# A two-block network in float32 on one core: float32 products of attention weights and values in block 2, a new order of the beginning, products of constants in waits, and late inputs of block 1 moved

## The chip, the core and the metric

The kernel runs on one core of one Trainium2 chip. TensorE (PE in the profile) makes the products, VectorE (DVE), ScalarE (ACT) and GpSimd (POOL) do the elementwise work, and SyncE (SP) issues nearly all DMAs. Each engine works off its instructions in one order that is fixed when the kernel is built. The metric is the time of one execution in microseconds (us), from the chip.

## What is computed

Two transformer-like blocks work on a latent sequence of 256 tokens (LAT) and a context of 256 tokens (CTX), both 1024 wide, in float32. Each block has two layers; each layer is an FFN, a mixer and a second FFN, and each of these three stands behind a norm that is scaled and shifted by "mods" (products of silu(c) with a large matrix). The mixers are a convolution of width 31, neighbourhood attention, attention with a latent key and value (MLA) beside windowed heads with a sink (SWA), and a state-space layer (S5).

```python
x = first_block(x, c, ctx, ...)          # FFN, conv, FFN; FFN, neighbourhood attention, FFN; norm
return second_block(x, c_2, ctx_2, ...)  # FFN, MLA + SWA, FFN; FFN, S5, FFN

def ffn_sublayer(h, m, j, g_pre, g_post, w13, w2):
    a = modulate(h, g_pre, m[3 * j], m[3 * j + 1])     # rmsnorm(h, g) * (1 + scale) + shift
    return h + FFN_RES * m[3 * j + 2] * rmsnorm(swiglu(a, w13, w2), g_post)

def softmax_attention(q, k, v, scale):
    s = jnp.einsum('bqhd,bkhd->bhqk', q, k) * scale
    return jnp.einsum('bhqk,bkhd->bqhd', jax.nn.softmax(s, axis=-1), v)
```

## The kernel before

All activations lie transposed, 1024 features as eight tiles of 128 partitions, 256 columns a stream. A product of two float32 matrices is made as three fast products of parts that were rounded beforehand: high times high, low times high, high times low (`mm`, L109, makes every product; `gemm` strings them together). ScalarE writes a high part (`hh` of activations at L693, `wh` of weights at L183, `th` in attention at L1587), VectorE the low one as the difference (`hl` L696, `wl` L188, `tl` L1588). Weights come in 1 MB pieces on SyncE's queue (`raw`), are converted, and wait in five slots; `pump` starts the next conversion when a slot comes free.

The stages follow one another: f100, conv, f102, f110, na, f112 of block 1, then f200, attn, f202, f210, s5, f212 of block 2 (an f is an FFN: pairs of gate and up tiles `gu`, then down tiles `pd`). Between two stages stands a norm: squares are summed up on ScalarE and VectorE, TensorE sums them over the partitions (`ssq`), GpSimd takes the power -1/2 (`rr`, L268), TensorE spreads it (`bc`), and VectorE and ScalarE make `nt`, `hh` and `hl`. Such steps are held in a `Chain` and sent in when a running clock of TensorE's work (`pe_t`) has gone on far enough; what is not sent by then is forced (`force`).

A `Task` is background work that is sent in the same way, a step for so many ns of TensorE's work. One of them, `pre` (`s5_pre`), makes the tables of S5 for eight d in two halves each, long before S5 needs them: rotations `E` (L2165 to L2172), `vw` (L2073 to L2085) and `ow` (L2110 to L2120) on GpSimd, small products `pvt` and `kp` on TensorE, copies on ScalarE and VectorE, and DMAs to tables `dE`, `dT`, `dK`, `dV`, `dO` in DRAM. It is handed to f100, f102 and f110 as `side`: an FFN starts it at its beginning and stops it at its end, and what is left is drained before na (L2511). The order on each engine is then set by a scheduler that takes instructions by the place in the program and by when a simulated clock says that they are ready.

In na (L1173) LAT's half of the projections `pq`, `pk`, `pv` comes first, CTX's behind it. A bias `vb` is loaded (L1232) and added to the values (`vt`, L1246). Behind na the second block's context is loaded into CTX's tile (L500). In conv TensorE does some of the taps with diagonal matrices `dgw` that ScalarE writes (L1004). In attn (L1531) `turn` transposes softmax weights and splits them into `th` and `tl`, and `pv` multiplies them by split values, three products for each pair of tiles.

Of the kernel before, what the change touches and what calls it, by code (L numbers as in the profile page):

```python
# [13 lines left out]
D = 1024  # L14
# [9 lines left out]
class Acc:  # L24
    def __init__(self, tag):
        self.tag, self.t, self.pend, self.ps = tag, None, None, None

# [9 lines left out]
class Chain:  # L37
    def __init__(self, k):
        self.k = k
        self.steps = []  # L40
        self.t0 = k.pe_t
        k.chains.append(self)
# [35 lines left out]
class Core:  # L78
    def __init__(self, ctx, tc, ap):
# [3 lines left out]
        self.n_mm, self.marks, self.pin = 0, [], None  # L83
        self.chains = []
# [16 lines left out]
        self.dma_max, self.dma_behind = 1 << 30, False  # L101
# [6 lines left out]
    def mm(self, out, lhsT, rhs, start, stop, cost, **kw):  # L108
# [7 lines left out]
        return ins  # L116

# [29 lines left out]
    def force(self, c):  # L147
        was, self.ticking = self.ticking, True
        c.force()
        self.ticking = was  # L150

# [18 lines left out]
    def pump(self):  # L170
        while self.n_cv < min(len(self.pieces), self.n_rel + NBUF):
# [71 lines left out]
    def rstd(self, ch, acc, ncol, eps, cb, d1=900, d2=1500, inv=None, parts=False, pin=0, keep=None):  # L243

        nc = self.nc
        if isinstance(acc, Acc):
            self.flush(acc)

        def s1():
# [19 lines left out]

            def s2():  # L270
                bc = self.psa.tile([128, 512], F32, tag="a", name="bc")
# [4 lines left out]
                cb(bc[:, :ncol * 128])  # L276
            ch.steps.insert(0, (d2, s2))
        ch.steps.append((d1, s1))

    def square(self, src, acc, first):  # L280
        if first:
# [190 lines left out]
class Net(Core):  # L472
    def setup(self):
# [3 lines left out]
        nc.sync.dma_start(out=self.vec, in_=ap["vecs"])  # L477
# [11 lines left out]
        self.x = {}  # L489
        self.acc = {}  # L490
        self.modv = {}
# [6 lines left out]
    def load_x(self, s, name):  # L498
        t = self.xp.tile([128, KT, T], F32, tag=f"x{s}", name=f"x{s}")
        self.nc.sync.dma_start(out=t, in_=self.ap[name])  # L500
        self.x[s] = t

# [47 lines left out]
    def begin(self, room):  # L550
# [13 lines left out]
        self.load_x(LAT, "x")  # L564
        self.load_x(CTX, "ctx")
        tl = {}

        def load(k):
            tl[k] = self.mwp.tile([128, D], F32, tag="mw", name="mw")
            nc.sync.dma_start(out=tl[k], in_=self.ap["mw1"][0, 8 + k])  # L570
            for i in range(2):
                nc.sync.dma_start(out=room[i][k].rearrange("p (j m) -> p j m", j=4), in_=self.ap["mshift"][k][:, 4 * i:4 * i + 4])
        self._dma()
        load(0)
# [5 lines left out]
        bcs, acc = {}, {}  # L580
        psh = [self.psm.tile([128, 512], F32, tag="m", name="psh"), self.psa.tile([128, 512], F32, tag="a", name="psh")]
        for s in S2:
            t = self.mwp.tile([128, D], F32, tag=f"cb{s}", name=f"cb{s}", bufs=1)
            for i in range(2):
                ps = self.psm.tile([128, 512], F32, tag="m", name="cbp")
                self.mm(ps, self.ones[0:1, :], room[i][6 + s][0:1, :], True, True, 858)
# [944 lines left out]
    def attn2(self, ready, finish):  # L1531
# [3 lines left out]
        with ExitStack() as es:  # L1535
# [200 lines left out]
            def pv(H, c):  # L1736
# [15 lines left out]
                if c == 2:  # L1752
                    low(1)
# [854 lines left out]
```

## Time and profile before

| | us |
|---|---|
| median of 3 runs | 3609.77 |
| lowest and highest | 3609.4, 3611.73 |
| profiled execution | 3612.36 |
| its span | 3610.5 |

The profile has the busy time of each engine, the chain of work that ended last (followed back from the last instruction, each step to what released it), groups of instructions by line, the timeline of one engine, and the busy time in windows of the span. PEclk is the granted clock of TensorE as a share of 2.4 GHz; it has two levels, 2.4 and 1.2 GHz. Times are us from the start of the span unless marked ns.

### The profile page before, as it was taken

Reading aid. Unit: us, or ns where it says so; the run is one execution under the profiler, and the core shown is the slowest. Engines: PE = TensorE matmul, PEld = TensorE weight load, DVE = VectorE, ACT = ScalarE, POOL = GpSimd, SP = SyncE. Lnnn points to the kernel's source line nnn. Section 1 sums busy time; section 2 is a strip of 40 time slices with the busy share of each in tenths; the row PEclk is TensorE's granted clock in tenths of the full one; section 3 lists DMA queues with packets and bytes.
Section 4 is the critical chain, followed back from the end, with each engine's and each line's share of the span. In section 5 each row is a group of like instructions: output and inputs, shape, how many; then the busy total and the mean of one; then the engine's idle time right before and its main releaser. Section 6 shows DMA issues by size and latency. Waiting matters only on the chain.

```text
span 3610.5 us, 54700 instructions
## 1 busy us (share of the span) xinstructions
PE 3482.7 (96%) x21248; PEld 3056.4 (85%) x21248; DVE 2590.3 (72%) x4487; ACT 1389.1 (38%) x2428; POOL 749.8 (21%) x870
## 2 busy tenths in 40 slices
PE   8999998999999999999999999889999999999898
PEld 7888867888898888989998889779888988897898
DVE  8987697876586765768987766878887633368655
ACT  4222444422242323554443234655322432244443
POOL 5100001577657772000000001211000100014000
PEclk9999999999999999999999999999999999999899
DMA  7555211455454774236755542014557332238353
GB/s 260 200 189 197 71 59 48 162 190 186 164 169 170 257 242 138 92 120 235 262 187 188 182 145 97 34 50 153 208 206 247 134 124 94 102 120 300 121 197 119
DMA packets 157835, 579.35 MB, mean 160 GB/s; under 512 B 25220, under 2 KB 56708, under 8 KB 117896
## 3 DMA queue, kind: packets, MB, share of 16 engines
q1 hardware_dynamic: 157576, 575.86, 45.8%
q8 instruction: 167, 2.74, 0.3%
q14 instruction: 92, 0.75, 0.1%
HBM read 546.50 MB, written 29.29 MB: 159 GB/s over the span
## 4 chain that ended last, share of the span: by engine, by line
PE 89%; DVE 7%; ACT 2%; issue 1%; POOL 1%; DMA 0%; SPq 0%; POOLq 0%; DVEq 0%; ACTq 0%
PE gu L109 46%; PE pd L109 24%; PE pj L109 8%; PE po L109 2%; PE ptap L109 1%; PE pv L109 1%; PE pk L109 1%; PE ps L109 1%; DVE wl L188 1%; PE ssq L109 1%; PE pT L109 1%; PE pq L109 1%; PE bc L109 1%; DVE ry L2291 0%; DVE jk L612 0%
## 5 line engine op out<-in xcount | busy, mean ns | idle before, releaser
L183 ACT ACTIVATE wh<-raw 128x1024 fp32r<-128x1024 f32 (+1 forms) x679 | 700.8, 1038 | 1581.4 <-PE gu L109 911.7
L188 DVE TENSOR_TENSOR wl<-raw,wh 128x1024 fp32r<-128x1024 f32 (+1 forms) x677 | 839.3, 1244 | 358.5 <-ACT wh L183 348.2
L109 PE MATMUL gu<-hl,wh 128*128 128x512 f32 (+1 forms) x3136 | 1083.8, 347 | 5.6 <-DVE hl L696 4.6
L109 PE MATMUL gu<-hh,wh 128*128 128x512 f32 (+1 forms) x3136 | 1076.9, 348 | 10.0 <-ACT hh L693 6.2
L109 PE MATMUL gu<-hh,wl 128*128 128x512 f32 (+1 forms) x3136 | 1082.0, 346 | 0.0
L538 DVE CUSTOM_DVE_ANT_0 jk<-mw,cb,vec 128x1024 bf16<-128x1024 f32 x480 | 639.0, 1331 | 73.2 <-DMA mw<-in_mw_dram 68.4
L109 PEld LDWEIGHTS gu<-hl,wh 128*128 128x128 f32 x3136 | 600.7, 192 | 78.2 <-DVE hl L696 6.0
L109 PEld LDWEIGHTS gu<-hh,wh 128*128 128x128 f32 x3136 | 596.9, 192 | 81.6 <-ACT hh L693 7.6
L109 PEld LDWEIGHTS gu<-hh,wl 128*128 128x128 f32 x3136 | 600.7, 192 | 70.3 <-issue 1.0
L109 PE MATMUL pd<-Hl,wh 128*128 128x256 f32 (+1 forms) x1696 | 561.8, 332 | 0.0
L109 PE MATMUL pd<-Hh,wl 128*128 128x256 f32 (+1 forms) x1696 | 561.0, 332 | 0.0
L109 PE MATMUL pd<-Hh,wh 128*128 128x256 f32 (+1 forms) x1696 | 559.0, 331 | 0.0
L268 POOL TENSOR_TENSOR rr<-rv,mhalf 128x2 f32<-128x2 f32 (+1 forms) x34 | 28.9, 850 | 1852.9 <-DVE rv L266 1796.4
L109 PEld LDWEIGHTS pd<-Hl,wh 128*128 128x128 f32 x1696 | 322.0, 190 | 30.2 <-issue 0.4
L109 PEld LDWEIGHTS pd<-Hh,wl 128*128 128x128 f32 x1696 | 321.9, 190 | 30.2 <-issue 0.4
L109 PEld LDWEIGHTS pd<-Hh,wh 128*128 128x128 f32 x1696 | 321.5, 190 | 29.9
L779 DVE TENSOR_TENSOR gu<-sg,gu 128x512 f32<-128x512 f32 (+1 forms) x196 | 113.4, 579 | 192.6 <-PE gu L109 191.6
L109 PE MATMUL pj<-hh,wh 128*128 128x256 f32 (+1 forms) x736 | 226.3, 322 | 15.4 <-ACT hh L693 9.0
L109 PE MATMUL pj<-hl,wh 128*128 128x256 f32 (+1 forms) x736 | 231.2, 318 | 1.1 <-DVE hl L1089 1.0
L109 PE MATMUL pj<-hh,wl 128*128 128x256 f32 (+1 forms) x736 | 228.5, 316 | 1.1 <-DVE wl L188 1.1
L109 PEld LDWEIGHTS pj<-hh,wh 128*128 128x128 f32 x736 | 142.0, 200 | 25.8 <-ACT hh L693 9.9
L109 PEld LDWEIGHTS pj<-hl,wh 128*128 128x128 f32 x736 | 146.8, 200 | 9.0 <-issue 1.7
(425 smaller groups left out, 4332.1 us busy)
## 6 DMA issues: line engine op xcount, KB each, us to landing
raw<-in_gu_dram SPq DMA_DIRECT2D x186, 1024.0 KB, 4.9
mw<-in_mw_dram SPq DMA_DIRECT2D x280, 512.0 KB, 4.6
raw<-in_dn2b_dram SPq DMA_DIRECT2D x38, 1024.0 KB, 4.7
raw<-in_dn1b_dram SPq DMA_DIRECT2D x32, 1024.0 KB, 5.3
raw<-in_dn1a_dram SPq DMA_DIRECT2D x16, 768.0 KB, 4.4
raw<-in_pw_dram SPq DMA_DIRECT2D x12, 1024.0 KB, 4.7
raw<-in_dn2a_dram SPq DMA_DIRECT2D x16, 768.0 KB, 4.3
dO<-ow SPq DMA_DIRECT2D x32, 256.0 KB, 2.6
```

The costliest lines, as they stand in the source:

```text
L109: ins = self.last_mm = self.nc.tensor.matmul(out=out, lhsT=lhsT, rhs=rhs, start=start, stop=stop, **kw)
L183: ins = nc.scalar.activation(out=h2, in_=r, func=AF.Copy)
L188: self.low_p = lambda eng=eng, l2=l2, r=r, h2=h2: eng.tensor_sub(l2, r, h2.bitcast(F32))
L268: nc.gpsimd.tensor_tensor(r[:, :ncol], v[:, :ncol], self.mhalf[:, :ncol], ALU.pow)
L538: self.behind_pe(nc.vector.tensor_tensor_reduce(out=jk, in0=tl[i], in1=self.cb[s], scale=1.0, scalar=self.V(f"mod_b{b}{l}")[:, j:j + 1], o ...
L779: nc.vector.tensor_mul(pr[:, :n], sg[:, :n], pu[:, :n])
```

## The change

Six things are edited; the diff is cut to its core.

- *Beginning.* x is loaded first, the vector table later; the norm steps of both streams are interleaved with the silus, and the first call of `pump` moves behind the first tile.
- *Products of constants.* `warm` puts float32 products of the 128 x 128 identity with itself into places where TensorE waits at norms: 112 in all.
- *`side`* starts in f102 and f110 ahead of the sixth tile pair.
- *conv.* The `dgw` activations are held behind what TensorE was last given.
- *na.* The bias's first load is written at the beginning of na, the load of `ctx_2` is held behind TensorE's last product, and `cv_max` puts off conversions of weights at na's end.
- *attn.* Transposed weights and values stay float32 and are multiplied in one float32 product; two heads share one tile, which is split once.

```diff
+    def warm(self, ps, ns, last=None):
+        for _ in range(int(ns / 215)):
+            ins = self.nc.tensor.matmul(out=ps[:, 256:384], lhsT=self.ident, rhs=self.ident, start=True, stop=True)
+            self.behind(ins, self.last_mm)
...
+            self.last_mm = self.pin = ins
...
+    def forced(self, c, late=0, least=0):
+        self.force(c, late)
+        if c.spare is not None:
+            self.warm(c.spare, max(1400 - (self.pe_t - c.t2), least), c.last)
...
@@ rstd
+                if self.late:
+                    self.warm(ps, 2800 + self.late - (self.pe_t - at))
...
             def s2():
+                n = 1700 - (self.pe_t - t1)
+                if at is not None and n > 215:
+                    self.warm(self.psa.tile([128, 512], F32, tag="a", name="idle"), n)
...
@@ begin
-        self.load_x(LAT, "x")
         self.load_x(CTX, "ctx")
+        nc.sync.dma_start(out=self.vec, in_=self.ap["vecs"])
...
+        sums(LAT)
+        first_step(ch[LAT])
+        silu(LAT)
+        sums(CTX)
+        self.force(ch[LAT])
+        first_step(ch[CTX])
+        silu(CTX)
+        shift(0)
+        self.force(ch[CTX])
+        scale(0)
         self.dma_max = 2
-        self.pump()
-        shift(0)
-        scale(0)
         for k in range(8):
...
+            if k == 0:
+                self.pump()
...
@@ ffn
             def background():
                 nonlocal task
-                if side is not None and not side.done:
+                if begin is not None and not side.done:
                     self.start(side)
...
-                            self.force(ready[s])
+                            self.forced(ready[s], late, 860 if two and b == 2 and s == streams[0] else 0)
+                            if self.cv_max < 1 << 30:
+                                self.cv_max = 1 << 30
+                                self.pump()
...
+                        if g == 0 and f == n1 + 1 and side is not None and not side.done and side not in self.tasks:
+                            self.start(side)
                         gu([(self.take(), self.take())], f, 0, N)
...
@@ conv
-                    nc.scalar.activation(out=dg, in_=self.ident, func=AF.Copy, scale=w(ek[len(dgs)]))
+                    self.behind_pe(nc.scalar.activation(out=dg, in_=self.ident, func=AF.Copy, scale=w(ek[len(dgs)])))
...
+                    if m == 1 and s == LAT:
+                        self.warm(ps, 1500)
...
@@ na
+            def vbias(g):
+                vb[g] = n2.tile([128, T], F32, tag="vb", name="vb", bufs=1)
+                nc.sync.dma_start(out=vb[g], in_=self.ap["vbias"][g * T:(g + 1) * T].partition_broadcast(128))
+            vbias(0)
...
+                self.cv_max = self.n_take + KT - 3 + 2
...
@@ joint_norm
+        self.warm(ps, 3600)
...
         for r in rs:
+            self.warm(self.psa.tile([128, 512], F32, tag="a", name="idle"), 1200 if r is rs[0] else 400)
...
+        self.warm(ps, 1500)
...
@@ attn2
-                split(th.rearrange("p a q -> p (a q)"), tl.rearrange("p a q -> p (a q)"), ps)
-                H["t", c] = (th, tl)
+                nc.scalar.activation(out=th.rearrange("p a q -> p (a q)"), in_=ps, func=AF.Copy)
+                H["t", c] = th
...
+                o = po[r:r + 64, :T] if c < 2 else po[r:r + 64, T:]
+                for i in range(2):
+                    self.mm(o, H["v"](2 * c + i if c < 2 else 2 + i), H["t", c][:, i, :], i == 0 and c != 1, i == 1 and c != 0, 429)
...
@@ s5
+                        if (b, m) == (0, 1) and d in (0, 7):
+                            self.warm(self.psa.tile([128, 512], F32, tag="a", name="idle"), 1900)
...
+        self.warm(self.psa.tile([128, 512], F32, tag="a", name="idle"), 1900)
         for d in range(2):
             glu_part(d, range(4, KT))
...
@@ network
-        self.load_x(CTX, "ctx_2")
+        self.behind_pe(self.load_x(CTX, "ctx_2"))
...
-        self.ffn(1, (LAT,), ready, gates(1, 1, 2, (LAT,)), final, work=(norm_and_mods(), 61))
+        self.ffn(1, (LAT,), ready, gates(1, 1, 2, (LAT,)), final, work=(norm_and_mods(), 61), late=1000)
```

How the order of instructions changes is shown at three places. A row has the line, the operation, out<-in with the program's names, the shape and a count. Lines are those of each kernel; before's L2110 to L2172 are L2165 to L2227 in the changed kernel. The first place is GpSimd's order at the end of f110 and the start of na. Before, the last rotations `E` of the tables are followed by six `rr` in a row, na's two for LAT and CTX among them:

```order
L2165 TENSOR_TENSOR pt_11686<-E_12266 128x8x31
L2166 TENSOR_TENSOR pt_11687<-E_12267 128x8x31
L2167 TENSOR_TENSOR E_12266<-pt_11686,pt_11687 128x8x31
L2170 TENSOR_TENSOR pt_11686<-E_12266,E_12267 128x8x31
L2171 TENSOR_TENSOR pt_11687<-E_12267,E_12266 128x8x31
L2172 TENSOR_TENSOR E_12267<-pt_11686,pt_11687 128x8x31
L268 TENSOR_TENSOR rr<-rv,mhalf 128x2 x6
L1555 MEMSET kbh_20797 32x512
```

After, the `rr` of LAT stands among table instructions; 84 of them stand between it and the `rr` of CTX, of which the next two pieces show the first and the last:

```order
L2138 TENSOR_TENSOR vw_11989<-pw_11653,bb_11742 128x512
L2140 TENSOR_TENSOR vw_11988<-vw_11988,vw_11989 128x512
L294 TENSOR_TENSOR rr<-rv,mhalf 128x2
L2165 TENSOR_TENSOR ow_12374<-pw_11652,bc 128x576
L2171 TENSOR_TENSOR ow_12375<-pw_11653,bc 128x576
L2208 MEMSET E_12399 128x8
L2211 COPY E_12399<-cc_1001 128x8
```

```order
L2175 TENSOR_TENSOR ow_12583<-ow_12583,ow_12584 128x576
L2209 MEMSET E_12608 128x8
L2211 COPY E_12608<-cs_1002 128x8
L294 TENSOR_TENSOR rr<-rv,mhalf 128x2
L2221 TENSOR_TENSOR pt_12464<-E_12608 128x8
L2222 TENSOR_TENSOR E_12607<-pt_12463,pt_12464 128x8
L2225 TENSOR_TENSOR pt_12463<-E_12607,E_12608 128x8
```

The tables' instructions moved from ahead of na's two `rr` to between and behind them.

The second place is SyncE's order around the first `vb`. Before, the stores `dE` of the last rotations stand ahead of two loads of na's weights (`raw`), and the bias is behind the tables' `tt` and `dT` and the context's load:

```order
L2180 DMA dE_158<-E_12267 128x256
L164 DMA raw<-in_naqk_dram 128x2048
L164 DMA raw<-in_nav_dram 128x2048
L2199 DMA dK_166<-kt 128x240
L2021 DMA tt<-dK_166 16x4x128 x8
L2023 DMA dT_174<-tt 128x512
L2021 DMA tt<-dK_166 16x4x128 x8
L164 DMA raw<-in_naqk_dram 128x2048
L2023 DMA dT_174<-tt 128x512
L500 DMA x_15165<-in_ctx_dram 128x2048
L1232 DMA vb<-in_vbias_dram 128x256
L1331 DMA nb<-in_nab_dram 128x512 x3
```

After, this is what stands ahead of the first `vb`:

```order
L2254 DMA dK_167<-kt 128x240
L2076 DMA tt<-dK_167 16x4x128 x8
L2078 DMA dT_175<-tt 128x512
L2076 DMA tt<-dK_167 16x4x128 x6
L2235 DMA dE_158<-E_12607 128x256
L2235 DMA dE_159<-E_12607 128x256
L2076 DMA tt<-dK_167 16x4x128 x2
L2235 DMA dE_158<-E_12608 128x256
L2235 DMA dE_159<-E_12608 128x256
L2078 DMA dT_175<-tt 128x512
L186 DMA raw<-in_naqk_dram 128x2048
L1288 DMA vb<-in_vbias_dram 128x256
L1396 DMA nb<-in_nab_dram 128x512 x3
```

The context's load has left the place ahead of `vb`, and the tables' stores `dE` of the last rotations (`E_12607`, `E_12608`) stand there.

The third place is ScalarE's order at conv's start. Before, 17 `dgw` stand between the third `hh` of LAT and the fourth:

```order
L693 ACTIVATE hh_95<-nt,mod_212 128x256
L285 ACTIVATE sq<-x_225 128x256
L183 ACTIVATE wh<-raw 128x1024
L1004 ACTIVATE dgw<-cst,vec 128x128 x17
L285 ACTIVATE sq<-x_225 128x256
L693 ACTIVATE hh_96<-nt,mod_212 128x256
L1004 ACTIVATE dgw<-cst,vec 128x128
L693 ACTIVATE hh_97<-nt,mod_212 128x256
```

After, the first `dgw` stand behind CTX's last `hh`:

```order
L743 ACTIVATE hh_100<-nt,mod_213 128x256
L743 ACTIVATE hh_101<-nt,mod_213 128x256
L743 ACTIVATE hh_94<-nt,mod_214 128x256
L1037 ACTIVATE t<-pj,hb_3373 128x256
L743 ACTIVATE hh_95<-nt,mod_214 128x256
L743 ACTIVATE hh_96<-nt,mod_214 128x256
L743 ACTIVATE hh_97<-nt,mod_214 128x256
L743 ACTIVATE hh_98<-nt,mod_214 128x256
L743 ACTIVATE hh_99<-nt,mod_214 128x256
L743 ACTIVATE hh_100<-nt,mod_214 128x256
L1035 ACTIVATE th<-pj,hb_3373 128x256
L743 ACTIVATE hh_101<-nt,mod_214 128x256
L1059 ACTIVATE dgw<-cst,vec 128x128 x8
```

The `dgw` moved behind all sixteen `hh` of conv's start.

## Rows read from the trace of the kernel before

**Rows 1.** The chain that ended last, shares of the span by engine

```profile
PE 89%; DVE 7%; ACT 2%; issue 1%; POOL 1%; DMA 0%; SPq 0%; POOLq 0%; DVEq 0%; ACTq 0%
```

**Rows 2.** Timeline, GpSimd, na's start: start, duration, engine, line, operation, count, [idle <-releaser]

```profile
1405.07 0.71 POOL L268 TENSOR_TENSOR rr<-rv,mhalf 128x2 f32<-128x2 f32 x1 [9.07 <-DVE rv L266]
1419.50 0.87 POOL L268 TENSOR_TENSOR rr<-rv,mhalf 128x2 f32<-128x2 f32 x1 [13.72 <-DVE rv L266]
```

**Rows 3.** GpSimd's busy time (x instructions), PEclk, DMA share, GB/s; timeline of rotations' ends

```profile
1312.00:1396.00 84.00, 57.33 (x82) 1.00 0.54 177
...
1376.01 0.21 POOL L2156 COPY E<-cc 128x8 f32<-128x8 f32 x1
...
1395.21 0.79 POOL L2172 TENSOR_TENSOR E<-pt,pt 128x248 f32<-128x248 f32 x1
```

**Rows 4.** Timelines of SyncE, VectorE and TensorE at the first `vb`

```profile
1432.91 0.42 SPq L1232 DMA_DIRECT2D vb<-in_vbias_dram  x1
...
1440.98 0.76 DVE L1246 TENSOR_TENSOR vt<-pv,vb 128x256 f32<-128x256 f32 x2 [2.62 <-DMA vb<-in_vbias_dram]
...
1441.46 0.58 PE L109 MATMUL pv<-wh,hh 128*128 128x256 f32 x1 [5.10 <-DVE vt L1246]
```

**Rows 5.** TensorE's groups by line, 640 to 1412: count | busy, mean ns | idle

```profile
L109 PE MATMUL pvt<-cst,vw 128*128 128x128 f32 x128 | 19.0, 271 | 0.0
L109 PE MATMUL kp<-ow,bbz 128*32 128x128 f32 x248 | 10.8, 279 | 0.0
```

**Rows 6.** Windows: length, TensorE's busy time (x instructions), PEclk, DMA share, GB/s

```profile
405.00:420.00 15.00, 10.70 (x72) 0.89 0.21 72
562.00:592.00 30.00, 21.90 (x97) 0.77 0.16 53
636.00:666.00 30.00, 22.68 (x141) 0.77 0.50 157
1052.00:1064.00 12.00, 10.00 (x71) 0.86 0.72 228
1622.00:1642.00 20.00, 13.11 (x82) 0.74 0.47 171
1849.00:1864.00 15.00, 12.04 (x78) 0.77 0.31 106
2260.00:2420.00 160.00, 137.34 (x845) 0.95 0.09 31
2459.00:2479.00 20.00, 16.10 (x103) 0.74 0.31 106
3240.00:3360.00 120.00, 103.71 (x1497) 0.90 0.65 229
3390.00:3412.00 22.00, 13.83 (x77) 0.69 0.24 89
```

**Rows 7.** GpSimd's window at f102's start; VectorE's `hl` in 636:666 and 670:700

```profile
636.00:666.00 30.00, 26.46 (x25) 0.77 0.50 157
...
L696 DVE SCALAR_TENSOR_TENSOR hl<-nt,mod,hh 128x256 fp32r<-128x256 f32 x8 | 7.8, 1026 | 0.0
...
L696 DVE SCALAR_TENSOR_TENSOR hl<-nt,mod,hh 128x256 fp32r<-128x256 f32 x8 | 3.6, 474 | 0.0
```

**Rows 8.** Timeline, ScalarE, conv's start

```profile
406.02 5.07 ACT L1004 ACTIVATE dgw<-cst,vec 128x128 f32<-128x128 f32 x17
```

**Rows 9.** VectorE's `tl` in attention; TensorE's timeline around float32 taps in conv

```profile
L1588 DVE TENSOR_TENSOR tl<-pT,th 128x512 fp32r<-128x512 f32 x48 | 31.6, 679 | 10.3 <-ACT th L1587 10.0
...
540.58 0.28 PE L109 MATMUL pj<-hh,wl 128*128 128x256 f32 x1
540.70 7.04 PE L109 MATMUL ptap<-u,dgw 128*128 128x512 f32 x16
547.18 0.68 PE L109 MATMUL pj<-hh,wh 128*128 128x256 f32 x1
```

**Rows 10.** VectorE's window in the beginning

```profile
20.00:60.00 40.00, 39.35 (x77) 1.00 0.73 261
```

More of the change, by code (lines that the diff above doesn't have):

```diff
@@ L276, in s2 @@
                 cb(bc[:, :ncol * 128])
+                if not ch.quiet:
+                    ch.spare, ch.t2, ch.last = spare, self.pe_t, self.last_mm
             ch.steps.insert(0, (d2, s2))
@@ L602, in begin, with silu, first_step @@
             pipe(KT, [square, add], 2)
+            ch[s] = Chain(self)
+            ch[s].quiet = True
+            self.rstd(ch[s], acc[s], 2, 1e-6, lambda bc, s=s: bcs.update({s: bc}))
+        def silu(s):
+            t = self.mwp.tile([128, D], F32, tag=f"cb{s}", name=f"cb{s}", bufs=1)
+            for i in range(2):
+                nc.scalar.activation(out=t[:, i * 512:i * 512 + 512], in_=cbp[s, i], func=AF.Silu)
+            self.cb.append(t)
+        def first_step(c):
+            was, self.ticking = self.ticking, True
+            c.step()
+            self.ticking = was
         def shift(k):
@@ L716, in plan_ffn, with ffn @@
                     self.plan(self.ap[f"dn{b}b"][l, i, g - 1, p], [8, 8])
-    def ffn(self, b, streams, ready, gate, after, nsplit=4, first=1, work=None, side=None, head=0, tail=0, begin=None):
+    def ffn(self, b, streams, ready, gate, after, nsplit=4, first=1, work=None, side=None, head=0, tail=0, begin=None, late=0):
         nc, tc = self.nc, self.tc
@@ L1230, in values @@
                     if g not in vb:
-                        vb[g] = n2.tile([128, T], F32, tag="vb", name="vb", bufs=1)
-                        nc.sync.dma_start(out=vb[g], in_=self.ap["vbias"][g * T:(g + 1) * T].partition_broadcast(128))
+                        vbias(g)
+                    if g not in v_:
                         v_[g] = [n2.tile([128, 4, T], F32R, tag=f"v{x}", name=f"v{x}") for x in "hl"]
@@ L1561, in attn2 @@
             a2 = es.enter_context(self.pool("at2", 2))
[L1562 removed]
+            vs = a2.tile([128, 4, 128], F32, name="vs", bufs=1)
             swcm = self.pool("sw")
@@ L1740, in pv @@
-                po = H["po"]
-                val = lambda c, i: H["v"](2 * c + i if c < 2 else 2 + i)
-                out = lambda c: po[:64, :T] if c < 2 else po[:64, T:]
-                def low(c):
-                    for i in range(2):
-                        self.mm(out(c), val(c, i)[0], H["t", c][1][:, i, :], False, i == 1 and c > 0, 109)
-                def high(c):
-                    for i in range(2):
-                        self.mm(out(c), val(c, i)[0], H["t", c][0][:, i, :], i == 0 and c != 1, False, 109)
-                        self.mm(out(c), val(c, i)[1], H["t", c][0][:, i, :], False, False, 109)
@@ L1752, in pv @@
-                if c == 2:
-                    low(1)
-                if c < 3:
-                    high(c)
-                if c == 1:
-                    low(0)
-                if c == 3:
-                    low(2)
-                    m, r = H["o"]
-                    split(self.hh[m][r:r + 64, :], self.hl[m][r:r + 64, :], po[:64, :])
+                m, r = H["o"]
+                if c == 0 and r == 0:
+                    pair[m] = self.psm.tile([128, 512], F32, tag="m", name="po")
```

77 lines of the change are left out of this document (41 added, 36 removed).

## The prediction, made before the changed kernel ran

> **What bounds the kernel now.** I read the chain that ended last first. It is TensorE for 89% of the span and VectorE for 7% [rows 1]; GpSimd and the DMA queues hardly show in it. So nearly all of the kernel is a stream of products that runs as fast as TensorE goes, and time can be won in two places: where TensorE stands idle, and where its granted clock is at the lower of its two levels, 1.2 instead of 2.4 GHz. Next I read TensorE's busy time and granted clock over the stretches that the change touches [rows 6]: a stretch's length less its busy time is idle time, and the length times (1 minus the clock) is the most that the clock can have cost in it. Then I looked at what each idle time waits for, at the order of the instructions on GpSimd, SyncE and ScalarE before and after, and at the small rows that price each moved instruction. The sum is made against the profiled execution (3612.36 us, span 3610.5), which lies 2.6 us above the median of the runs shown; I take these 2.6 us off at the end.
>
> **Part 1, the tables of S5 start later (the loss).** The task that builds S5's tables (GpSimd, with small products, copies and DMAs) now starts in f102 and in f110 only ahead of the sixth tile pair instead of at the start. It is paced by TensorE's work, so it is late by what ten pairs take, and by the new order two and a half of its sixteen half passes are left when f110 ends; they are drained in front of na. GpSimd's queue is in order. In the kernel before, na's two norm steps `rr` stand next to each other, and GpSimd is idle for 13.72 us ahead of the second (1419.50) [rows 2]. In the changed order 84 table instructions stand between them. A whole d of the same tables was 57.33 us of busy time in 82 instructions, 8 of which are memsets of another task of about 0.31 us each; 54.8 us for 74 [rows 3]. Ten more at that mean (0.74) give 62 us. The first `rr` ended at 1405.8, so the second starts near 1468, 48 us later than before, and CTX's half of the projections, which needs its result, cannot begin before that.
>
> The bias `vb` is hit harder. SyncE's queue is in order too, and `vb` now stands behind the stores of the last rotations, which GpSimd finishes only after that `rr`: 20 us for the rotations (1376.01 to 1396.0) [rows 3], about 2 us for the half dozen DMA issues in front of it (0.4 each by the row of `vb` [rows 4]), then the load. Before, `vb` was issued at 1432.91 and its first use started at 1440.98, 8.1 us later, behind a 1 MB load of `ctx` that the change moves away; without it I take 5 us, between nothing and 8. So the first use comes at 1468 + 1 + 20 + 2 + 5 = 1496, 55 us later than 1440.98. TensorE was waiting for just this at 1441.46 (5.10 us idle) [rows 4], and everything behind it follows. LAT's half covers none of this: it is over in both kernels long before, and the DVE rows that need `vb` hold the rest of VectorE's queue. What is given back: about two and a half of the sixteen half passes of small products move from f110, where they cost time, into the wait; 2.5/16 of 29.8 us [rows 5], 4.7 us, which leaves **50 us lost**. Bounds: 36 if the 84 take only 50 (a part of the 54.8 was contention with VectorE) and `vb` lands in 3; 70 if LAT's own `rr` too waits for the eleven table instructions just ahead of it (8 us), `vb` takes 8 and the 62 grow by a seventh.
>
> What the same delay gives: at f102's start VectorE makes h while GpSimd is 26.46 us of 30 busy, and one `hl` takes 1026 ns there against 474 a little later [rows 7]. TensorE is idle for 7.3 us of these 30, and the clock costs up to 6.9 [rows 6]. Without GpSimd's work beside it I expect 9 us back of 14.2 (between 4 and 14). At f110's start 2 of 3.7 us.
>
> A rule of the Trainium skill bears on this: by "SBUF — State Buffer", section "SBUF: two separate sides", GpSimd and VectorE share a pair of ports as an exclusive lock, held for a whole instruction, when VectorE reads two inputs from SBUF. The doubled `hl` agrees with it. The rule also speaks against the change: the same lock would now be fought over at na's start, where VectorE makes CTX's h while GpSimd works off its 84 instructions. If they lengthen there by a sixth, as an estimate, the 62 us become 72 and the time 10 us longer than I say.
>
> **Part 2, conv's start.** Seventeen `dgw` activations (5.07 us) stood on ScalarE ahead of the `hh` that TensorE waits for [rows 8]; TensorE was idle for 4.3 us there and the clock cost up to 1.65 [rows 6]. In the new order they stand behind all `hh`. The first product that reads one stands well behind conv's first projections in TensorE's order, which hide them. I take 5 us (2 to 6); next is VectorE's own h.
>
> **Part 3, constants' products in waits.** 112 products of 128 x 128 in float32 are put into waits around norms. Each takes about 0.2 us at the high clock (a 512-column one takes 6.48/8 = 0.81 us [rows 9]), so 22 us of work, twice that at the low clock. In an idle time they cost nothing; what they can give is a clock that stays up, and what they can cost is the overhang behind the input that the real product waits for. The most that the clock can give by [rows 6] is 6.9 (conv's end), 5.2 (f112), 3.45 (f200, and the same at attention's and S5's starts), 5.2 (f202), 12 (S5's outputs) and 6.8 (f212). The waits themselves stay, since VectorE's sums and ScalarE's h end them. As the clock was lost in waits of a few us that are only partly filled, I take some two fifths: conv's end 2, f112 5 (with 1 or 2 for weights converted later), the three starts 6, f202 3, S5 3, f212 3: **22 us**. Bounds: -5, if products overhang and the clock falls all the same, and 40.
>
> **Part 4, attention.** 288 split products of 256 columns give way to 96 in float32. One split product takes 0.12 us and one in float32 of 256 columns 6.48/16 = 0.405 [rows 9], so TensorE gets 38.9 for 34.6: 4 us more. VectorE loses 48 subtractions of 679 ns, 32.6 us [rows 9], and a few smaller ones. TensorE was idle for 22.7 us of 160 here and the clock cost up to 8 [rows 6]. VectorE is nearly as full as TensorE there, so I take a third of these 30 as given back and the 4 us off: about **4 us** won (-7 to 14).
>
> **Part 5, the beginning.** x is loaded ahead of other inputs and the norms start earlier, but VectorE is busy for 39.35 of the 40 us from 20 to 60 [rows 10], and the conversions that move behind the first step stand in the same queue. I take nothing (-2 to 3).
>
> **The sum.** Gains: 9 + 2 + 5 + 22 + 4 = 42. Loss: 50. Net 8 us longer: 3612.4 + 8 - 2.6 = **3618 us**, 0.23% above the median.
>
> **The rivals.**
> 1. *The drained tables cost less than the starts give, so the kernel is faster.* Its place is na's start. For it: the loss may lie at its lower bound, 36, and the gains of the two FFN starts, the clock and attention near their upper ends, 65 together. It decides as soon as the gains pass the loss. Against it: only the order of queues enters the loss, and it is fixed. Time: 3610 + 36 - 65 = 3581.
> 2. *Both sides come out at about 43 us.* Time: 3610.
> 3. *The constants' products don't hold the clock.* They fill only a part of each wait, and the granted clock falls all the same, or they overhang the input. Then the change does not do what it says in part 3, its 22 us shrink to nothing and some of the attention's gain with them. Time: 3618 + 24 = 3642. For it: most waits at norms are of 1 to 5 us, and a product of constants is also queued ahead of the real one.
>
> **How the numbers follow.** A measurement of this kernel can tell about 0.2%, 7 us, from no change. My forecast (0.40) spreads 10 us to both sides, so 0.23 of it is slower by more and 0.17 within. Rival 1 has 0.27, all faster. Rival 2 has 0.10, within. Rival 3 has 0.23, all slower. Faster 0.27, same 0.27, slower 0.46. The range has to reach into rivals 1 and 3: from 3586 to 3647.
>
> **What would show it.** In the trace of the changed kernel: the two `rr` of na on GpSimd about 60 us apart, with table instructions between; TensorE idle for some 40 us or more in na's first 90 us; `vb` issued last after the stores of the rotations; na's length up by 50 us. At f102's start `hl` near 0.47 us and TensorE's idle time below 3 us. ScalarE's `dgw` behind `hh` and no 4 us wait at 407. A granted clock near 1.00 at f112, f200, f202 and f212 would show part 3 right, at 0.75 as before would show it wrong. In attention 48 subtractions fewer and TensorE's idle time below 15 of 160 us. I am wrong if GpSimd's tables are done before na begins, or if na's wait is there and the rest of the kernel gives back more than it.

## The result and the profile after

The changed kernel takes 3637.68 us (median of 4 runs, 3636.35 to 3638.07) against 3609.76 (3609.4 to 3611.73): a ratio of 1.0074 with an interval of 1.0062 to 1.0087, 28 us longer. The profiled execution took 3638.07 us, its span is 3636.3.

From the page of the changed kernel, busy times and the chain that ended last by engine:

```profile
PE 3511.6 (97%) x21376; PEld 3058.7 (84%) x21376; DVE 2533.0 (70%) x4426; ACT 1383.5 (38%) x2420; POOL 735.4 (20%) x870
...
PE 88%; DVE 5%; POOL 2%; issue 2%; ACT 1%; DMA 0%; SPq 0%; POOLq 0%; DVEq 0%; ACTq 0%
```

TensorE's share of the chain fell from 89% to 88% and VectorE's from 7% to 5% [rows 1], GpSimd's is 2% now. TensorE is busy for 97% of the span: that the kernel is longer is not to be seen in such an average. It is seen by setting the start of the same product in the two timelines side by side, before and after (one execution of each kernel was traced). The differences, after less before, at the ends of the stages:

| from here to there | difference at the end, us | gained (-) or lost (+) there |
|---|---|---|
| start to f100's first tiles (60) | +3.3 | +3.3 |
| conv's start (405 to 440) | +1.0 | -2.3 |
| rest of conv (to 625) | +0.2 | -0.8 |
| f102's first 90 us | -11.5 | -11.7 |
| f110's start (1030 to 1112) | -17.9 | -6.4 |
| na's start (1405 to 1470) | +33.0 | +51.0 |
| rest of na | +32.2 | -0.8 |
| f112's start, then the rest of f112 | +30.2, +31.1 | -2.0, +0.9 |
| f200 | +31.6 | +0.5 |
| attention's start and projections (2195 to 2250) | +30.1 | -1.5 |
| attention (to 2440) | +29.1 | -1.0 |
| f202's start (to 2510) | +35.5 | +6.3 |
| f210's start | +33.9 | -1.6 |
| S5 with its start | +27.1 | -6.8 |
| f212's start, and to the end | +25.8 | -1.3 |

**na.** The timeline of GpSimd at na's start (start, duration, engine, line, operation, count), to be set against [rows 2]:

```profile
1387.06 0.71 POOL L294 TENSOR_TENSOR rr<-rv,mhalf 128x2 f32<-128x2 f32 x1 [26.87 <-DVE rv L292]
...
1451.03 0.71 POOL L294 TENSOR_TENSOR rr<-rv,mhalf 128x2 f32<-128x2 f32 x1
```

The two `rr` are 64 us apart, 14.4 before. The other rows of that place, SyncE's and VectorE's timelines at the first `vb`, what TensorE waited for in 1383 to 1490 (us in total, times, longest), and its window (length, busy time, granted clock, DMA share, GB/s):

```profile
1470.56 0.45 SPq L1288 DMA_DIRECT2D vb<-in_vbias_dram  x1
...
1476.39 0.76 DVE L1310 TENSOR_TENSOR vt<-pv,vb 128x256 f32<-128x256 f32 x2 [11.20 <-DMA vb<-in_vbias_dram]
...
PE pvt L112 <- POOL vw L2132: 26.4, 2, 24.2
PE pk L112 <- DVE vt L1310: 6.9, 1, 6.9
PE pvt L112 <- POOL vw L2140: 6.3, 2, 4.9
...
1405.00:1490.00 85.00, 41.71 (x234) 0.66 0.40 120
```

TensorE waited 26.4 and 6.3 us for the tables' `vw`, which the small products `pvt` read that stand in its own order ahead of CTX's projections, and 6.9 us for `vt`, whose bias was issued at 1470.56 and used at 1476.39 (8.1 us from issue to use before, 5.8 now). In 85 us TensorE was busy for 41.71, at a mean clock of 0.66.

**f102.** GpSimd's window, VectorE's `hl` and TensorE's window in 636 to 666, for [rows 7] and the third row of [rows 6]:

```profile
636.00:666.00 30.00, 1.54 (x1) 0.94 0.45 159
...
L746 DVE SCALAR_TENSOR_TENSOR hl<-nt,mod,hh 128x256 fp32r<-128x256 f32 x15 | 6.5, 482 | 0.2 <-ACT hh L743 0.2
...
636.00:666.00 30.00, 28.08 (x217) 0.94 0.45 159
```

GpSimd has 1.5 us of work there instead of 26.46, `hl` takes 482 ns instead of 1026, and TensorE is idle for 1.9 us instead of 7.3. A part of the 11.7 and 6.4 us of the table is work that only moved: the small products `pvt` and `kp` took 3.1 us of TensorE's time at f102's start and 3.9 at f110's before, and take nothing and 1.2 now.

**The other places.** TensorE's windows at the places of [rows 6], each moved by the difference of the table, with f202 in two pieces:

```profile
407.00:422.00 15.00, 13.43 (x86) 0.89 0.20 72
562.00:592.00 30.00, 22.14 (x101) 0.77 0.16 53
1040.00:1052.00 12.00, 11.93 (x99) 1.00 0.35 130
1652.00:1672.00 20.00, 19.03 (x163) 1.00 0.71 270
1881.00:1896.00 15.00, 12.01 (x75) 0.77 0.31 105
2291.00:2451.00 160.00, 150.75 (x762) 0.99 0.08 30
2490.00:2510.00 20.00, 16.92 (x121) 0.83 0.30 105
2510.00:2540.00 30.00, 24.76 (x180) 0.83 0.42 141
3271.00:3391.00 120.00, 108.45 (x1603) 0.97 0.68 242
3419.00:3441.00 22.00, 17.36 (x142) 1.00 0.16 59
```

The clock is at its full level now at f110's, f112's and f212's starts (0.86, 0.74 and 0.69 before) and nearly so in attention and in S5. At conv's end and f200's start it is 0.77 as before. At f202's start it is 0.83 for 50 us, where before 20 us at 0.74 were followed by 1.00: what TensorE waited for there, and GpSimd's adds of the residual in that place:

```profile
PE bc L112 <- POOL rr L294: 4.1, 1, 4.1
...
L1520 POOL TENSOR_TENSOR x<-x,pn 128x256 f32<-128x256 f32 x6 | 8.2, 1397 | 9.4 <-DVE pn L1516 9.4
```

### The profile page after: what moved, and what is told of

The parts are those of the page before. It is cut to its first block, busy times and chain, and to the rows that moved or that the text cites. A ratio compares the mean times of both kernels' runs of the same rounds, so it can differ in the third digit from the quotient of the medians.

```text
span 3636.3 us, 54874 instructions
## 1 busy us (share of the span) xinstructions
PE 3511.6 (97%) x21376; PEld 3058.7 (84%) x21376; DVE 2533.0 (70%) x4426; ACT 1383.5 (38%) x2420; POOL 735.4 (20%) x870
## 4 chain that ended last, share of the span: by engine, by line
PE 88%; DVE 5%; POOL 2%; issue 2%; ACT 1%; DMA 0%; SPq 0%; POOLq 0%; DVEq 0%; ACTq 0%
PE gu L112 46%; PE pd L112 22%; PE pj L112 8%; PE po L112 2%; PE ps L112 1%; PE ptap L112 1%; PE pk L112 1%; PE pv L112 1%; PE pT L112 1%; DVE wl L210 1%; PE ssq L112 1%; PE pq L112 0%; DVE ry L2346 0%; PE bc L112 0%; PE pqn L112 0%
```

## The experiments

Each run's median stands with its ratio to the kernel before on the same chip in the same sitting. side_early, only_side_late, late_1150 and vb_const share a sitting, in which the kernel before took 3613.40 us; no_constants, only_dgw, only_attention and begin_old share a second (3609.34), late_no202, three_edits and before_shift a third (3608.99), and late_noconst is of a fourth (3609.15). So the difference of two medians from different sittings is uncertain by a few us, and the places at which two traces part say more.

**side_early**, the changed kernel with the tables started as before.

```diff
-                if begin is not None and not side.done:
+                if side is not None and not side.done:
                     self.start(side)
...
-                        if g == 0 and f == n1 + 1 and side is not None and not side.done and side not in self.tasks:
-                            self.start(side)
```

> The changed kernel, but the tables of S5 start at the beginning of f102 and f110 as before. Theory A, the lateness of the tables makes the whole loss at na's start: na is 50 us shorter, f102 and f110 give their 17 us back, 3637.7 - 50 + 17 = 3605 us (3599 to 3611). Rival B, the moved bias, the moved context load and the held-back conversions make na longer: na stays as long and f102 and f110 lose their 17 us, about 3654 us.

3601.98 us (3600.57 to 3602.72), 0.997 of before (0.9958 to 0.9981): 36 us less than the changed kernel, as theory A said. GpSimd's two `rr` of na in this run:

```profile
1403.38 0.72 POOL L294 TENSOR_TENSOR rr<-rv,mhalf 128x2 f32<-128x2 f32 x1 [9.29 <-DVE rv L292]
1417.81 0.87 POOL L294 TENSOR_TENSOR rr<-rv,mhalf 128x2 f32<-128x2 f32 x1 [13.72 <-DVE rv L292]
```

They are next to each other again, 14.4 us apart. f102's start keeps 0.8 us of its 11.7 and f110's 1.1 of 6.4: GpSimd is busy again for 27.57 of f102's 30 us, and `hl` takes 1026 ns. Rival B falls.

**only_side_late**, the kernel before with the late start alone (the same edit the other way round).

> The kernel before with one edit, the late start of the tables in f102 and f110. Theory A: 17 us won in the two FFN stages and 50 us lost in na, 3609.8 + 33 = 3643 us (3637 to 3649), so slower than the whole change. Rival B: only the 17 us are seen, 3593 us.

3636.97 us, 1.0072 (1.0059 to 1.0086). One edit of six makes the whole loss: up to na's end this run differs from before as the changed kernel does (-17.8 at 1405, +33.1 at 1470). At f102's start GpSimd has 0.69 us of work and `hl` takes 481 ns. From na to the end the run comes 8 us nearer, 7.4 of them in S5, where nothing is edited in it; more on that below.

**late_1150**, the changed kernel with a faster pace for the tables.

```diff
-PRE_STEP = 1500
+PRE_STEP = 1150
```

> The changed kernel with the tables' step sent in every 1150 ns of TensorE's work in place of 1500, so that the late tables are done before na begins. Theory A: the 50 us at na's start go and the 17 us of the late start stay, 3588 us (3582 to 3596). Rival C: the faster pace lays GpSimd against VectorE more densely inside the two FFNs and gives the 17 us back there, 3605 us.

3592.70 us (3588.91 to 3596.70), 0.995 (0.9936 to 0.9963), 45 us less than the changed kernel. The two `rr` of na, and GpSimd's busy time within f102 and f110 (680 to 1020 and 1070 to 1380):

```profile
1393.86 0.71 POOL L294 TENSOR_TENSOR rr<-rv,mhalf 128x2 f32<-128x2 f32 x1 [30.75 <-DVE rv L292]
1407.51 0.87 POOL L294 TENSOR_TENSOR rr<-rv,mhalf 128x2 f32<-128x2 f32 x1 [12.94 <-DVE rv L292]
...
680.00:1020.00 340.00, 276.81 (x321) 1.00 0.54 179
1070.00:1380.00 310.00, 230.37 (x275) 1.00 0.63 213
```

The same windows of the kernel before:

```profile
680.00:1020.00 340.00, 239.84 (x286) 1.00 0.52 174
1070.00:1380.00 310.00, 213.02 (x242) 1.00 0.63 213
```

All tables are done before na and the starts of f102 and f110 stay short (12.1 and 6.7 us won). But the bodies of the two FFNs are longer: from 720 to 1030 and from 1112 to 1405 this run loses 4.1 and 4.4 us, where the changed kernel loses nothing. So a half of the 17 us is given back, as rival C said, but not by rival C's cause. TensorE is busy there for 339.66 of 340 us and 308.31 of 310, at a clock of 1.00, and waits for GpSimd for 2.0 us only. The rest is its own small products: 30.0 us of them lie here between the first pairs and na, and 23.5 in the changed kernel, which had put the other 6.5 into na's wait. The rows of this run (640 to 1410), then of the changed kernel (640 to 1385):

```profile
L112 PE MATMUL pvt<-cst,vw 128*128 128x128 f32 x128 | 19.3, 273 | 2.0 <-POOL vw L2140 2.0
L112 PE MATMUL kp<-ow,bbz 128*32 128x128 f32 x256 | 10.7, 279 | 0.0
...
L112 PE MATMUL pvt<-cst,vw 128*128 128x128 f32 x104 | 15.5, 271 | 0.0
L112 PE MATMUL kp<-ow,bbz 128*32 128x128 f32 x192 | 8.0, 279 | 0.0
```

**vb_const**, the changed kernel with the first bias loaded at the kernel's beginning into a room of its own.

```diff
+        self.vb0 = self.const.tile([128, 256], F32, name="vb0")
...
-                vb[g] = n2.tile([128, T], F32, tag="vb", name="vb", bufs=1)
-                nc.sync.dma_start(out=vb[g], in_=self.ap["vbias"][g * T:(g + 1) * T].partition_broadcast(128))
+                vb[g] = self.vb0 if g == 0 else n2.tile([128, T], F32, tag="vb", name="vb", bufs=1)
+                (nc.scalar if g == 0 else nc.sync).dma_start(out=vb[g], in_=self.ap["vbias"][g * T:(g + 1) * T].partition_broadcast(128))
```

> The changed kernel, but the first bias vb has a room of its own and is loaded at the kernel's beginning, so that it no longer stands behind the tables' stores; the norm's rr on GpSimd stays where it is. If rr and vb each make a part of the wait (theory A): TensorE's 6.9 us wait for vt and the low clock behind it go, about 10 us, 3628 us. If vb alone set the end of the wait: 50 us, 3588 us. If rr alone did: no change, 3638 us.

3637.55 us, 1.007 (1.0057 to 1.0084): no change. It would be wrong to read it as "only `rr` counts". Up to 1487 in the changed kernel's time this run is 15 us ahead, and 5 us later it is 0.5 behind. What TensorE and VectorE waited for, and SyncE's queue:

```profile
PE pT L112 <- ACT pt L1420: 11.4, 1, 11.4
...
DVE pt L1412 <- DMA nb<-in_nab_dram: 4.9, 1, 4.9
...
1472.30 0.34 SPq L2079 DMA_DIRECT2D dT<-tt  x1
1472.68 0.44 SPq L186 DMA_DIRECT2D raw<-in_naqk_dram  x1
1473.22 1.45 SPq L1397 DMA_DIRECT2D nb<-in_nab_dram  x3
```

TensorE now waits 11.4 us for softmax weights `pt`, and these for `nb`, the position bias, the next load in SyncE's queue behind the tables' last store. The second half of the wait belongs to the queue and not to the one load that the prediction named.

**no_constants**, the changed kernel without the 112 products (`warm` does nothing).

```diff
-        for _ in range(int(ns / 215)):
+        for _ in range(0):
```

> The changed kernel without the 112 products of constants. If they keep the clock up as the prediction took it (22 us): 3660 us. Read from the two traces, f112's start came 2 us nearer, f210's 2, S5 6 and f212 1, while f202's start went 6 us the other way: by that only 5 us, 3643 us. If what the clock does at these places hangs on how the waits happen to lie and not on the constants (S5 and f210 came as much nearer in the run with the late tables alone): no change within 4 us, 3634 to 3642 us.

3636.98 us, 1.0075 (1.0063 to 1.0088): the 112 products are worth nothing in the changed kernel. Its TensorE windows at f112's, f202's (second piece) and f212's starts:

```profile
1652.00:1672.00 20.00, 12.93 (x82) 0.74 0.70 270
2510.00:2540.00 30.00, 28.66 (x238) 1.00 0.39 134
3419.00:3441.00 22.00, 15.11 (x87) 0.69 0.13 48
```

So the products did what they say at f112 and f212: 1.00 with them, 0.74 and 0.69 without. But side by side with the changed kernel the higher clock gave only about 2 us at f112 and 1 at f212. The gain at f112 is firm: against the kernel before, that start wins 2.8 us in all six kernels here that have the products, and between -0.8 and 0.7 in the seven without. The most was won at attention's start (4), 1 each in attention and in S5; 7 were lost at f202 and 1.5 at f210. At f202 TensorE is busy for 28.66 us at 1.00 without them and for 24.76 at 0.83 with them.

**late_no202**, late_1150 without the four products at f202's start.

```diff
-        for _ in range(int(ns / 215)):
+        for _ in range(int(ns / 215) if self.marks[-1][1] != "f202" else 0):
```

> The changed kernel with the tables' step sent every 1150 ns (as in the run late_1150) and without the four constants' products at f202's start. Between the changed kernel and the one without any constants, f202's start lay 7 us apart, with a 4.13 us wait for a norm there only where the constants are. If these four make that wait: about 7 us less than late_1150, 3586 us, and no 4 us wait at f202's start. Rival, the wait comes from how the faster TensorE meets CTX's norm and mods whatever stands there: no change, 3592 us.

3585.22 us (3582.82 to 3590.39), 0.9937 (0.9924 to 0.9951), **the lowest median of all** and 7.5 us below late_1150's. The two lie in different sittings and their runs overlap (late_1150 from 3588.91); side by side the two traces part by 5.0 us at f202's start, and that much the four products cost there. TensorE's window 2460 to 2490 of late_1150, then 2440 to 2460 and 2460 to 2490 of this run:

```profile
2460.00:2490.00 30.00, 24.75 (x192) 0.89 0.36 123
```

```profile
2440.00:2460.00 20.00, 16.04 (x104) 0.74 0.39 147
2460.00:2490.00 30.00, 29.06 (x242) 1.00 0.41 141
```

The wait of 4.1 us and the low clock behind it are gone, though the clock at the start itself (the first of the two rows) is lower than with the products. They stand ahead of CTX's `ssq` in TensorE's queue; with them the mods' `jk` on VectorE come in between CTX's `pn`, and GpSimd's adds `x` take 1397 ns each (the row above; 1401 in late_1150) instead of 799 in the kernel before and 800 here, so that CTX's second norm ends after LAT's work that was to hide it. Against the kernel before, f202's start loses 2.3 to 6.3 us in all five kernels that have the four products, and between -0.8 and 0.4 us in the eight without. That the products start this is shown; how much of it is due to `jk` was not tried.

**late_noconst**, late_1150 without any of the products.

```diff
-PRE_STEP = 1500
+PRE_STEP = 1150
...
-        for _ in range(int(ns / 215)):
+        for _ in range(0):
```

> The run late_1150 without any of the 112 constants' products. If they are worth nothing net here as in the changed kernel (no_constants): 3592 us, and with f202's 7 us counted apart the others are worth 7, so 7 us more than late_no202. If they are worth the 22 us of the prediction where no other wait takes the gain: 3607 us or more.

3597.17 us, 0.9964 (0.995 to 0.9978). By the medians the other 108 products are worth 12 us against late_no202, and with f202's four 4.5 against late_1150: between the two expectations. All three runs are of different sittings; by the ratios it is 10 and 5 us, by the traces 14 and 9. Of the 14, 5.7 lie in S5, where kernels with nothing edited differ as much (below).

**only_dgw**, the kernel before with `dgw` held back alone.

```diff
-                    nc.scalar.activation(out=dg, in_=self.ident, func=AF.Copy, scale=w(ek[len(dgs)]))
+                    self.behind_pe(nc.scalar.activation(out=dg, in_=self.ident, func=AF.Copy, scale=w(ek[len(dgs)])))
```

> The kernel before with the diagonals held back alone. By the prediction TensorE's 4.25 us wait at conv's start goes and 5 us with it, 3605 us. Rival: conv is held by VectorE's taps afterwards, so that part of it comes back as waits there, 2 to 3 us, 3607 us.

3595.38 us (3594.34 to 3603.26), 0.9968 (0.9955 to 0.9980), 14 us less than before. By the side-by-side starts 3.9 us are won in conv, and most of that stays until na. The profiled execution is 17 us shorter than that of before; the other 13 come at na's start (2.7), in attention (1.8), f210 (3.1) and S5 (5.7), where nothing is edited. Two of the five runs took 3602.89 and 3603.26 us, the other three 3594.34 to 3595.38: 8 us come and go from run to run of this one kernel, so of the 14 us only those in conv are the edit's for certain.

**only_attention**, the kernel before with the float32 products alone.

```diff
-                split(th.rearrange("p a q -> p (a q)"), tl.rearrange("p a q -> p (a q)"), ps)
-                H["t", c] = (th, tl)
+                nc.scalar.activation(out=th.rearrange("p a q -> p (a q)"), in_=ps, func=AF.Copy)
+                H["t", c] = th
...
+                for i in range(2):
+                    self.mm(o, H["v"](2 * c + i if c < 2 else 2 + i), H["t", c][:, i, :], i == 0 and c != 1, i == 1 and c != 0, 429)
```

> The kernel before with the float32 products of softmax weights and values alone. By the prediction 4 us less than before (between 14 less and 7 more), 3606 us. Rival: TensorE's added work and the same waits cancel, no change within 2 us. In the trace 48 subtractions of VectorE fewer and attention's TensorE busy time 4 us up.

3604.48 us (11 runs, 3600.49 to 3610.59), 0.9987 (0.9978 to 0.9996): 5 us less, 2.4 are won in attention itself; by its profiled execution 5.8 more come in S5, which is not edited. TensorE's window in attention:

```profile
2258.00:2418.00 160.00, 151.90 (x769) 0.98 0.09 31
```

**begin_old**, the changed kernel with the old beginning.

```diff
-        sums(LAT)
-        first_step(ch[LAT])
-        silu(LAT)
-        sums(CTX)
-        self.force(ch[LAT])
-        first_step(ch[CTX])
-        silu(CTX)
...
+        for s in S2:
+            ch = Chain(self)
+            ch.quiet = True
+            self.rstd(ch, acc[s], 2, 1e-6, lambda bc, s=s: bcs.update({s: bc}))
+            self.force(ch)
```

> The changed kernel with the old order of the beginning. The prediction took the new order for nothing; by the trace it costs 3 us by 45 us into the run. If that is real: 3 us less than the changed kernel, 3634.5 us. Rival: the 3 us are made up before conv ends, as VectorE waits there: 3637.5 us.

3636.80 us, 1.0074 (1.006 to 1.0087). It is 2.5 us ahead of the changed kernel until na, still 1.3 ahead after na, and level at the end.

**three_edits**, the kernel before with the late start at the faster pace, `dgw` and the float32 products.

```diff
-PRE_STEP = 1500
+PRE_STEP = 1150
...
-                if side is not None and not side.done:
+                if begin is not None and not side.done:
...
-                    nc.scalar.activation(out=dg, in_=self.ident, func=AF.Copy, scale=w(ek[len(dgs)]))
+                    self.behind_pe(nc.scalar.activation(out=dg, in_=self.ident, func=AF.Copy, scale=w(ek[len(dgs)])))
...
-                H["t", c] = (th, tl)
+                H["t", c] = th
```

> The kernel before with three edits only: the late start of the tables in f102 and f110 with a step every 1150 ns, the diagonals of conv held back, and the float32 products in attention. No constants' products, the old beginning, na as before. If the other edits are worth nothing together: as late_1150, 3592 us, or by the single runs' sums 3609 - 17 - 4 - 5 = 3583 us. If the constants and the new beginning bring what the prediction gave them once the tables are out of the way: 20 us more than late_1150, 3612 us.

3598.40 us (3592.13 to 3600.80), 0.9967 (0.9955 to 0.9978), neither the sum of the single runs (3583) nor 20 us more than late_1150. The trace shows where the sum fails. It had counted the 17 us whole, but the two FFNs win 12.0 and 6.7 us at their starts and give back 4.0 and 5.8 in their bodies, much as in late_1150; conv wins 2.6 us instead of 3.9, and attention with its start wins nothing of its 2.4.

**before_shift**, the kernel before with 17 constants' products where TensorE waits for nothing.

```diff
         self.n_mm += 1
+        if self.n_mm == 1500:
+            ps = self.psa.tile([128, 512], F32, tag="a", name="idle")
+            for _ in range(17):
+                more = self.nc.tensor.matmul(out=ps[:, 256:384], lhsT=self.ident, rhs=self.ident, start=True, stop=True)
+                self.behind(more, self.last_mm)
+                self.last_mm = self.pin = more
```

> The kernel before with 17 constants' products (3.6 us at the high clock) in the middle of f100's down products, where TensorE waits for nothing; all that comes later is later by as much. If a time lost or won is simply carried on: 3609.3 + 3.6 = 3613 us, and the same low-clock stretches at the same waits. If the places where the clock falls hang on when the waits come: a total that differs from that by 5 us or more, with low-clock stretches longer or shorter at waits that nothing was edited at.

3608.41 us (11 runs, 3601.84 to 3611.65), 0.9995 (0.9986 to 1.0003). It is 4.1 us behind up to attention, as expected, and then 1.8 are won in attention, 3.1 at f210 and 1.9 later, so that it ends 3.1 ahead. TensorE's windows at f202's and f210's starts in this run, and f210's in the kernel before:

```profile
2459.00:2479.00 20.00, 15.98 (x111) 0.83 0.40 150
2845.00:2860.00 15.00, 12.87 (x106) 1.00 0.66 264
```

```profile
2841.00:2856.00 15.00, 12.85 (x91) 0.89 0.73 281
```

The clock is 0.83 (0.74 in [rows 6]) and 1.00 (0.89) at starts that nobody touched. By the medians the added 3.6 us don't come through: carried on they would give a ratio of 1.0010, outside the interval, though the total lies 4.2 us from 3612.6 and not the 5 that were asked for. That the shift chose other waits for the clock to fall in is not shown by it. The kernel before alone spread over 10 us in this sitting, at mean clocks of 0.979 (3613.68) to 0.982 (3605.89), so the 7 us between these two traces may be the difference of two executions of one kernel.

## Why the prediction came out as it did

**The side was right, the size not.** 8 us longer was said, 28 measured, within the range. It lies near rival 3's 3642 us, whose chance was 0.23 and up to which the range had been drawn.

**Part 1, the loss at na: right, a little too large.** 54.7 said, less 4.7 for small products given back: 50. Measured are 51.0 between 1405 and 1470, to be set against the 54.7, since what is given back stands in f102 and f110 (5.8). That 51.0 lies so near the 50 is chance. The 62 us for GpSimd's 84 instructions were 63.3 (from the end of the first `rr` to the start of the second), the 5 us for `vb` 5.8. What the mechanism left out: TensorE's own order puts the small products `pvt` ahead of CTX's projections, and most of the wait is theirs; and behind `vb` stands `nb` in the same queue. Neither changed the sum, since all hang on the same 84 instructions and the same stores.

**The gain at f102 and f110: near what was said.** 9 and 2 said, 11.7 and 6.4 measured; without the small products that moved, 3.1 and 2.7, it is 8.6 and 3.7. `hl` at 482 ns and idle time of 1.9 us show the mechanism as it was said, and side_early and only_side_late switch it off and on. The Trainium skill's "SBUF — State Buffer" (section "SBUF: two separate sides") agrees with the halved `hl`. What the prediction feared from it for na did not come about: VectorE's work of CTX's norm fell behind the last of the 84, beside the rotations' short instructions (0.2 to 0.6 us each), and `hl` took 485 ns there.

**Part 2, `dgw`: 5 said, 2.3 measured** at conv's start, 3.9 in all of conv in only_dgw. The 4.25 us wait went. ScalarE's and TensorE's rows at that place:

```profile
424.03 1.26 ACT L1059 ACTIVATE dgw<-cst,vec 128x128 f32<-128x128 f32 x4
...
411.21 0.50 PE L112 MATMUL pj<-hh,wh 128*128 128x256 f32 x2 [0.30 <-ACT hh L743]
412.92 0.27 PE L112 MATMUL ssq<-invd,acc 128*128 128x1 f32 x1 [1.21 <-DVE acc L329]
```

What is next there is the wait of 1.2 us for VectorE's sums in the last row.

**Part 3, the constants: the step that failed.** 22 us said, 0 by the run without them. Side by side with it the changed kernel wins some 10 us in six places and loses as much in four. Two things were wrong in the term. A higher clock was taken as time that comes back: at f112 it went from 0.74 to 1.00 over 20 us, 5 us by that and 5 said, and 2 came back; at f212 3 were said and 1 came. Why not more was not tried apart (the making of h by VectorE and ScalarE behind a norm may hide the rest). And the waits were treated as if the constants had nothing behind them: at f202 four of them cost 7 us by no_constants and 5 by late_no202, where 3 were to be won. Rival 3 came about in part: the clock was not held at conv's end and at f200 (0.77 as before), and at f202 products in front of another input cost time; at f112 and f212 it was held, and most of the gain failed all the same. The result lies within the term's bounds (-5 to 40), and beyond f202's four the products were worth some 10 us where the tables were out of the way.

**Part 4, attention: 4 said, 1 measured** in the changed kernel and 2.4 alone. By the prediction's own terms, a third of 30 less 4, it should have said 6. The float32 products cost more than 0.405 us each; two of them stand in the profile as four rows:

```profile
2333.70 1.08 PE L112 MATMUL po<-th,vs 128*64 128x256 f32 x4
2334.71 0.50 PE L112 MATMUL ps<-kzh,qsh 128*128 128x512 f32 x1
```

From their start to that of the next product these two take 1.01 us; four in a row take 1.87 and six 2.74, so 0.43 each and some 0.14 us more for each group. All 96 take 47.1 us in this way, 12.5 more than the 34.6 of the split ones and not 4. VectorE's relief was larger than taken, too: TensorE's idle time in 160 us fell from 22.7 to 9.3, by 13.4 where a third of 30 was said. Both terms were too small, and their errors nearly cancel; that the net came near is luck.

**Part 5, the beginning: 0 said, 3.3 lost** (2.5 by begin_old). VectorE's window 20 to 60 is no longer full, as [rows 10] was:

```profile
20.00:60.00 40.00, 34.83 (x68) 0.91 0.62 223
...
33.66 0.51 PE L112 MATMUL gu<-hh,wl 128*128 128x512 f32 x1 [1.89 <-DVE wl L210]
```

TensorE waits there for converted weights, whose first conversions had moved behind the first step (the second row). The total hardly shows it: begin_old ends level with the changed kernel.

**S5: 3 said and 2 for its start, 6.8 measured**, but only_side_late wins 7.4 there and no_constants 5.6, with no product of constants in either, so the most of it isn't their doing. All thirteen kernels traced here win 2.0 to 7.8 us in S5 and its start against the one trace of the kernel before, before_shift too. So a part of it may belong to that one execution; a second trace of the kernel before was not taken, and this stays open.

By the profiled executions the change is 25.7 us longer, 17.8 more than the 8 of the sum: f202 9.3, conv and f112 3.9 each, the beginning 3.3, attention 3, the starts of f200 and attention 3, f212 1.7 and na 0.2 on the one side, f102 and f110 7.1, S5 1.8 and f210 1.6 on the other.

## What to carry to other kernels

When background work starts later, count what is left of it where it is drained, and count the instructions that then stand between two steps of the next stage on each in-order queue: here 84 on GpSimd and the stores behind them cost nearly three times what the late start had won, and a faster pace kept a good part of the gain without the loss. Work that is put off is to be counted where it lands: a third of the late start's gain was TensorE's own small products, which came back later. Work put into a wait must be weighed by who stands behind it in that queue, and a higher clock is not worth the whole of its time: here 5 us gave 2. Gains of a few us are to be read at the place, from the same instruction in both traces, and in more than one kernel: totals also move by up to 10 us through waits that nobody edited.

## What was not expected of the hardware

- 3.6 us of added work left the total where it was (ratio 0.9995); in the two traces the clock at unedited starts went from 0.74 to 0.83 and from 0.89 to 1.00.
- The time of one kernel moves from run to run with its mean granted clock: the kernel before took 3604.82 us at 0.981 and 3618.01 at 0.979, only_dgw 3594.34 at 0.983 and 3602.89 at 0.980. The changed kernel's four runs lie within 3636.35 to 3638.07; whether it would spread as far in more runs was not tried.
- Float32 products with 64 output rows and 256 columns took 0.43 us each in a row, but 0.50 in groups of two among split ones, against 0.405 for 256 columns of the 512-column taps as read from [rows 9].
